# Hyena's output projection in the gates' rings: yh's split in hT's first half, the last two gate chunks as one group, two more gate chunks left for the attention

## The chip, the cores and the metric

The kernel runs on one core of a Trainium2 chip. The metric is the device time of one execution in microseconds (us), the median of several runs. The engines are PE (TensorE, matrix products), DVE (VectorE), ACT (ScalarE), POOL (GpSimd) and SP (SyncE, which here only issues DMAs). All data are fp32; the large products are each made of three passes over halves of a split operand (hi and lo).

## The reference

One block over 1024 latent tokens of width 1024, with 256 context tokens. Cut to what matters:

```python
h = modulate(rmsnorm(x, norm1_g), sh1, sc1)
q, k, v, hv, hx1, hx2, gna, ghy = split(h @ w_in)          # 5120 columns = 40 chunks of 128
y_na = neighbourhood_attention(q, k, v, k_ctx, v_ctx, rpb)
y_hy = hyena_mixer(hv, hx1, hx2, ...)                      # filters, then 2 long convolutions
m = sigmoid(gna) * (y_na @ w_na_o) + sigmoid(ghy) * (y_hy @ w_hy_o)
x = x + g1 * (m @ w_out)
x = x + g2 * swiglu(modulate(rmsnorm(x, norm2_g), sh2, sc2))
return rmsnorm(x, final_g)
```

Chunks 0 to 3 of the input projection are q, 4 to 11 k and v, 12 to 23 the Hyena inputs, 24 to 31 the gate gna, 32 to 39 the gate ghy.

## The kernel before

Everything is held with features on the 128 partitions and tokens along the free axis; a chunk is 128 features by 1024 tokens, done in two halves of 512 tokens. hT is the normed input, split into hTh and hTl, 8 x 128 features by 1024 tokens.

*Input projection* (`project`, L562). Per half of a chunk there are 24 matmuls (`gemm`, L186: 8 slices of features by three passes) into a bank `in_ps`, an eviction by ACT into a tile `proj` (a ring of two), and after the second half a store to DRAM, for a gate the scratch `gate`. Chunk weights are loaded (`weights`, L177: one raw buffer `wr`, two split pairs `wh`, `wl`) one chunk ahead.

*Side phase* (L946). The 40 chunks are the filler of a generator `side` that holds the Hyena filters (`filters`, L336: four sets, each of four steps that load decay tiles `dec`, multiply on PE into `filt_ps` and scale on DVE into `fv`, and then transforms `dft_ps`), the rows of the modulation (`ada_rows`, `ar_ps`), and four convolutions (`conv`, L437: DVE butterflies, PE transforms `dft_ps`). `_merged` (L138) picks by weights: side has SIDE = 447 steps against 39 for the projection, so a larger SIDE gives fewer chunks by the time that side ends. When the last convolution is reached, `fine` makes the projection go in halves.

*Attention* (`attention`, L649). 32 items (a pair of heads by 8 x 16 windows of the latent grid) in a pipeline: PE makes scores `s_ps` of item n, transposes the weights of item n-1 (`pt_ps<-ident,pe`) and multiplies the values of item n-2 (`pt_ps<-pts,v`); DVE and ACT make the softmax between. The biases of an item's scores are two loads of 192 KB on SP into four buffers. First AHEAD = 5 halves of chunks go alone, then each item is followed by one half of what is left (L959), twelve halves, items 0 to 11.

*Hyena's output projection* (`hyena_out`, L823). After the last half, hT's pool and the projection's weights are closed, and new pools take their place: `wf`, `ya`, `hyo` and one bank `ps1`. The Hyena output yh comes back from DRAM as eight loads `yhraw` of 256 KB, through a ring of two buffers (tag g), and is split into yhh and yhl. Then 16 halves (8 chunks f by 2) of 12 matmuls `hy_ps`, each multiplied by the stored gate (`ghy`, 256 KB loaded to the same ring) and stored to the scratch `hyo`. L978 says which items of the attention get one: not items 12 to 14, and from then on three of four.

*Mix* (`mix`, L1026). For each of eight chunks f: 2 x 12 matmuls `na_ps`, the gates `gate` and `hyo` loaded and combined into mh, ml; and the output weight `wor` (512 KB), multiplied by the row g1. Two chunks at a time go through `out_ps`. The eight x tiles are loaded behind the second chunk's gates. Its pools w4 and w4b stand on the side where the attention's stood.

Each engine runs its instructions in the order in which the program was written, except where a scheduler moves instructions ahead by priority; SP's queue is one order of all loads, and a load waits at its head until its buffer is free.

Of the kernel before, what the change touches and what calls it, by code (L numbers as in the profile page):

```python
# [18 lines left out]
P = 128  # L19
# [4 lines left out]
SIDE = 447  # L24
# [134 lines left out]
class Block:  # L159
# [17 lines left out]
    def weights(self, pool, src, n=D, tag="w"):  # L177
        nc = self.nc
        raw = pool.tile([P, n], F32, tag=tag + "r", name=tag + "r")
        nc.sync.dma_start(raw, src)  # L180
        hi = pool.tile([P, n], F32R, tag=tag + "h", name=tag + "h")
        lo = pool.tile([P, n], F32R, tag=tag + "l", name=tag + "l")
        self.split(hi, lo, raw)
        return hi, lo
# [74 lines left out]
    def hidden(self, pool, wpool, mp, hid, w3, hT, hcT, psf):  # L259
# [42 lines left out]
        self.modulated(pool, psf, xs[0:4], 4, self.mod1[:, 0], hT[0][:, :, 0:512], hT[1][:, :, 0:512])  # L302
        normed(4, 4, "rstd1b")
        yield
        self.modulated(pool, psf, xs[4:8], 4, self.mod1[:, 0], hT[0][:, :, 512:T], hT[1][:, :, 512:T])
# [256 lines left out]
    def project(self, groups, wpool, psg, psc, hT, hcT, between):  # L562
# [8 lines left out]
        def half(f, w, st, ps, h):  # L571
# [4 lines left out]
            self.gemm(pt, w, hT, 8, 512, h * 512, self.pinned)  # L576
# [50 lines left out]
        for group in groups:  # L627
            ws = [self.ready.pop(f) for f in group]
            i = chunks.index(group[-1]) + 1
            if i < len(chunks) and chunks[i] not in self.ready:  # L630
                with self.tc.high_priority():
                    self.ready[chunks[i]] = self.weights(wpool, self.a["w_in"][chunks[i]])
            sts = [self.stg.tile([P, T], F32, tag="o", name="proj") for _ in group]
            pss = [[] for _ in group]
            for h in range(2):
                for f, w, st, ps in zip(group, ws, sts, pss):
                    half(f, w, st, ps, h)
                if self.fine and not h:
                    yield
                if group is groups[0]:  # L640
                    next(between)
            for f, w, st in zip(group, ws, sts):
                self.left -= 1
                finish(f, w, st)
                yield
# [240 lines left out]
    def run(self):  # L886
        tc, nc, a = self.tc, self.nc, self.a
        with ExitStack() as top:
# [74 lines left out]
            with ExitStack() as s3:  # L963
# [7 lines left out]
                with ExitStack() as s4:  # L971
# [8 lines left out]
                    for _ in hyena:  # L980
                        pass
# [447 lines left out]
```

## Time and profile before

| what | value |
|---|---|
| time, median of 3 runs | 1749.97 us (1749.7 to 1755.51) |
| the profiled execution | 1746.28 us, its span 1744.5 us |
| PE busy | 1671.1 us, 96% of the span |
| DVE, ACT, POOL busy | 1187.9, 661.6, 157.9 us |
| granted PE clock, mean | 0.989 |
| filters, modulation rows | to about 303 us |
| convolutions beside chunks | 303 to 686 us |
| attention with input chunks, then Hyena chunks | 696 to 948 us |
| mix and FFN | 948 us to the end |

The stages are read from the first and last starts of their tiles. A busy time counts instructions that run on the engine, not the time in which it waits; an engine at 96% leaves 73 us in which it stands idle, over all stages. The table says nothing of where these are; the rows below do.

### The profile page before, as it was taken

The numbers are of one execution on the slowest core, as the hardware profiler recorded it, in microseconds if no ns is written. First come the engines' busy times: TensorE is split into PE (matmuls) and PEld (weight loads), VectorE is DVE, ScalarE is ACT, GpSimd is POOL, SyncE is SP. The second block draws the span as 40 slices with busy tenths as digits, with TensorE's granted clock in tenths as the row PEclk, the third lists the DMA queues.
The fourth block names the chain that finished last, engine by engine and source line by source line (L and its number), as shares of the span: only waits on it lengthen the run. The fifth ranks groups of instructions, "written<-read, shape, count | busy, mean of one in ns | idle before, by whom it ended". The sixth has DMA issues, their size and how long they took to land.

```text
span 1744.5 us, 22924 instructions
## 1 busy us (share of the span) xinstructions
PE 1671.1 (96%) x8348; PEld 1315.6 (75%) x8348; DVE 1187.9 (68%) x2004; ACT 661.6 (38%) x1143; POOL 157.9 (9%) x281
## 2 busy tenths in 40 slices
PE   5999999999999999998999999899999999999997
PEld 2766766777777777787777888688888888877886
DVE  4556266699795855655965867968765656479567
ACT  4611222312221213545654225633343333344555
POOL 0100210101000004002200000000100000100000
PEclk8999999999999999999999999999999999999999
DMA  8376556645454427435747524233423322395344
GB/s 344 116 248 199 182 180 222 210 147 179 138 203 160 160 100 223 135 109 165 218 146 247 167 67 168 110 116 126 139 91 101 103 98 97 108 374 180 99 121 151
DMA packets 110758, 281.20 MB, mean 161 GB/s; under 512 B 15535, under 2 KB 24371, under 8 KB 108341
## 3 DMA queue, kind: packets, MB, share of 16 engines
q1 hardware_dynamic: 90584, 218.68, 37.9%
q0 software_dynamic: 19408, 60.61, 10.2%
q8 instruction: 66, 1.08, 0.3%
q10 hardware_dynamic: 653, 0.44, 0.1%
q14 instruction: 47, 0.39, 0.1%
HBM read 212.28 MB, written 67.39 MB: 160 GB/s over the span
## 4 chain that ended last, share of the span: by engine, by line
PE 67%; issue 13%; DMA 9%; DVE 6%; ACT 3%; POOL 1%; SPq 0%; ACTq 0%; POOLq 0%; DVEq 0%
PE in_ps L194 22%; PE x_ps L1133 9%; PE dx_ps L1297 5%; PE dft_ps L430 5%; PE z_ps L1133 4%; PE out_ps L1071 4%; PE dz_ps L1297 3%; PE dft_ps L431 2%; PE dft_ps L432 2%; PE na_ps L194 2%; DMA w<-in_w 2%; DMA wal<-in_w_ada 2%; PE y_ps L1133 1%; PE dy_ps L1297 1%; PE ctx_ps L194 1%
## 5 line engine op out<-in xcount | busy, mean ns | idle before, releaser
L194 PE MATMUL in_ps<-hTh,wl 128*128 128x512 f32 x640 | 257.8, 404 | 3.6 <-ACT proj L601 3.6
L194 PE MATMUL in_ps<-hTl,wh 128*128 128x512 f32 x640 | 252.7, 395 | 0.0
L194 PE MATMUL in_ps<-hTh,wh 128*128 128x512 f32 x640 | 252.2, 395 | 0.0
L194 PEld LDWEIGHTS in_ps<-hTh,wl 128*128 128x128 f32 x640 | 121.3, 190 | 34.8 <-issue 5.9
L194 PEld LDWEIGHTS in_ps<-hTh,wh 128*128 128x128 f32 x640 | 121.2, 189 | 26.8 <-issue 1.2
L194 PEld LDWEIGHTS in_ps<-hTl,wh 128*128 128x128 f32 x640 | 121.3, 189 | 25.6 <-issue 1.2
L175 DVE TENSOR_TENSOR wl<-wr,wh 128x1024 fp32r<-128x1024 f32 x40 | 48.9, 1222 | 80.4 <-ACT wh L174 80.2
L175 DVE TENSOR_TENSOR ol<-ws,oh 128x512 fp32r<-128x512 f32 x88 | 60.6, 689 | 55.1 <-ACT oh L174 54.9
L174 ACT CAST wh<-wr 128x1024 fp32r<-128x1024 f32 x40 | 41.9, 1047 | 139.4 <-PE in_ps L194 111.2
L175 DVE TENSOR_TENSOR ol<-ar,oh 128x512 fp32r<-128x512 f32 x77 | 53.0, 689 | 49.0 <-ACT oh L174 49.0
L174 ACT CAST oh<-ar 128x512 fp32r<-128x512 f32 x77 | 47.9, 622 | 84.0 <-PE dx_ps L1297 34.7
L174 ACT CAST oh<-ws 128x512 fp32r<-128x512 f32 x88 | 54.7, 622 | 54.3 <-PE x_ps L1133 23.9
L1297 PE MATMUL dx_ps<-ol,oh 128*128 128x512 f32 x176 | 68.7, 391 | 1.7 <-DVE ol L175 1.7
L1297 PE MATMUL dx_ps<-oh,ol 128*128 128x512 f32 x176 | 67.1, 391 | 3.3 <-DVE ol L175 3.3
L754 DVE CUSTOM_DVE_ANT_0 pe<-s_ps,bias 128x640 f32<-128x640 f32 x64 | 50.1, 819 | 29.1 <-PE s_ps L749 29.1
L1297 PE MATMUL dx_ps<-oh 128*128 128x512 f32 x176 | 68.5, 389 | 0.0
L430 PE MATMUL dft_ps<-a,matf 128*128 128x512 f32 x128 | 66.1, 598 | 1.8 <-issue 1.1
L175 DVE TENSOR_TENSOR ol<-wr,oh 128x512 fp32r<-128x512 f32 x70 | 48.1, 690 | 28.8 <-ACT oh L174 28.7
L755 ACT ACTIVATE pe<-pe,mx 128x640 f32<-128x640 f32 x64 | 52.6, 823 | 37.5 <-DVE mx L754 37.4
L174 ACT CAST oh<-wr 128x512 fp32r<-128x512 f32 x70 | 43.1, 621 | 55.3 <-PE y_ps L1133 18.2
L1073 DVE TENSOR_TENSOR x<-x,out_ps 128x512 f32<-128x512 f32 x64 | 43.1, 685 | 18.7 <-PE out_ps L1071 18.5
L358 DVE TENSOR_TENSOR fv<-filt_ps,dec 128x512 f32<-128x512 f32 x32 | 21.6, 690 | 48.4 <-DMA dec<-in_decay 30.7
(392 smaller groups left out, 4225.4 us busy)
## 6 DMA issues: line engine op xcount, KB each, us to landing
wr<-in_w SPq DMA_DIRECT2D x50, 512.0 KB, 3.4
wr<-in_w_in SPq DMA_DIRECT2D x40, 512.0 KB, 4.5
ar<-g SPq DMA_DIRECT2D x77, 256.0 KB, 2.8
wal<-in_w_ada SPq DMA_DIRECT2D x32, 512.0 KB, 4.8
g<-t POOLq DMA_DIRECT2D x49, 256.0 KB, 3.0
matf<-in_dft_f SPq DMA_DIRECT2D x32, 384.0 KB, 4.3
bias<-in_rpb SPq DMA_DIRECT2D x64, 192.0 KB, 3.1
w<-in_w SPq DMA_DIRECT2D x44, 256.0 KB, 5.4
```

Of the source, the lines that this page charges most:

```text
L174: self.nc.scalar.copy(hi, src)
L175: self.nc.vector.tensor_sub(lo, src, hi.bitcast(F32))
L194: mm = nc.tensor.matmul(ps, ww[:, k * P:(k + 1) * P], xx[:, k, pos:pos + width], start=(i == 0), stop=(i == n - 1))
L430: nc.tensor.matmul(ps, m[:, 0], v.rearrange("p a b -> p (a b)"), start=True, stop=False)
L431: nc.tensor.matmul(ps[:, 0:256], m[:, 1], v[:, 1], start=False, stop=False)
L432: nc.tensor.matmul(ps[:, 256:512], m[:, 2], v[:, 0], start=False, stop=True)
L754: nc.vector.tensor_tensor_reduce(pe, ps[:, 256:896], bt, -1.0, 3e38, ALU.add, ALU.min, mx[:, 0:1])
L755: nc.scalar.activation(pe, pe, AF.Exp, bias=mx[:, 0:1], scale=-1.0, accum_out=mx[:, 1:2])
L1071: nc.tensor.matmul(ps, gg[x][:, tk], ww[y][:, sl], start=(i == 0), stop=(i == n - 1))
L1073: nc.vector.tensor_add(x1[:, sl], x1[:, sl], ps)
L1133: mm = nc.tensor.matmul(ps, w[u][:, k * P:(k + 1) * P], x[v][:, k, :], start=(start and k == 0 and i == 0), stop=(stop and k == 3 and i == 2),
L1297: nc.tensor.matmul(ps[j], x[u][:, j * P:(j + 1) * P], w[v], start=(start and i == 0 and c == 0), stop=(stop and i == N - 1 and k == len(re ...
```

## The change

1. hT is two tiles, one for each 512 tokens, in two pools: h1 (tokens 512 to 1023) and h0 (tokens 0 to 511).
2. The last two gate chunks, 30 and 31, form one group: first halves of both, then second halves of both. After the first halves nothing reads h0 any more, and `then` starts the loads of yh into h0's place, under the second halves.
3. `yhraw` goes through the ring of `tm` in the staging pool (two buffers), the gate of a Hyena chunk through the ring of `proj`, as one load of 512 KB (`ghy`), and is stored as one of 512 KB. The weights of Hyena's chunks and of `na_ps` go through the input weights' ring, `hy_ps` through the bank of `in_ps`.
4. ya, the attention's output split, is put where h1 was; pools `wf`, `hyo`, `ps1` fall away, and g1 gets a pool of its own that opens after the last Hyena half.
5. Each attention item from the one after the last gate half on gets one Hyena half, until there are none.
6. SIDE is 483: the chunks are spread more thinly over the steps of side, and four halves more are left for the attention, sixteen in all (items 0 to 15) beside the five alone.

The diff, cut to its core:

```diff
-SIDE = 447
+SIDE = 483
...
-            self.gemm(pt, w, hT, 8, 512, h * 512, self.pinned)
+            self.gemm(pt, w, hT[h], 8, 512, 0, self.pinned)
...
             for h in range(2):
                 for f, w, st, ps in zip(group, ws, sts, pss):
                     half(f, w, st, ps, h)
-                if self.fine and not h:
-                    yield
+                    if self.fine:
+                        if h:
+                            self.left -= 1
+                            finish(f, w, st)
+                        yield
                 if group is groups[0]:
                     next(between)
-            for f, w, st in zip(group, ws, sts):
-                self.left -= 1
-                finish(f, w, st)
-                yield
+                if group is groups[-1] and not h:
+                    then()
...
-    def hyena_out(self, pool, wo, ps1):
+    def hyena_out(self, pool, wpool, ps1):
...
-        yh = [pool.tile([P, 4, T], F32R, name=n, bufs=1) for n in ("yhh", "yhl")]
+        yh = [pool.tile([P, 8, 512], F32R, tag=n, name=m).rearrange("p (c h) t -> p c (h t)", h=2)
+              for n, m in (("hTh", "yhh"), ("hTl", "yhl"))]
         for c in range(4):
             for h in range(2):
                 sl = slice(h * 512, (h + 1) * 512)
-                raw = pool.tile([P, 512], F32, tag="g", name="yhraw")
+                raw = self.stg.tile([P, 4, P], F32, tag="tm", name="yhraw").rearrange("p a b -> p (a b)")
                 nc.sync.dma_start(raw, self.yhd[c][:, sl])
                 self.split(yh[0][:, c, sl], yh[1][:, c, sl], raw)
         yield
+        w = self.weights(wpool, a["why"][0], 512)
         for f in range(8):
-            w = self.weights(wo, a["why"][f], 512, "wf")
+            g = self.stg.tile([P, T], F32, tag="o", name="ghy")
+            nc.sync.dma_start(g, self.gd[8 + f])
             for h in range(2):
                 sl = slice(h * 512, (h + 1) * 512)
-                ps = ps1.tile([P, 512], F32, tag="f", name="hy_ps")
+                ps = ps1.tile([P, 512], F32, tag="g", name="hy_ps")
                 self.gemm(ps, w, yh, 4, 512, h * 512, True)
-                g = pool.tile([P, 512], F32, tag="g", name="ghy")
-                nc.sync.dma_start(g, self.gd[8 + f][:, sl])
-                nc.vector.tensor_tensor(g, ps, g, op=ALU.mult)
-                nc.gpsimd.dma_start(self.hyd[f][:, sl], g)
+                nc.vector.tensor_tensor(g[:, sl], ps, g[:, sl], op=ALU.mult)
+                if h:
+                    nc.gpsimd.dma_start(self.hyd[f], g)
+                    if f < 7:
+                        w = self.weights(wpool, a["why"][f + 1], 512)
                 yield
...
-                order = [[4, 5]] + [[f] for f in list(range(6, 24)) + list(range(4)) + list(range(32, 40)) + list(range(24, 32))]
+                order = [[4, 5]] + [[f] for f in list(range(6, 24)) + list(range(4)) + list(range(32, 40)) + list(range(24, 30))]
+                order.append([30, 31])
...
+                self.ya = [t.rearrange("p (c h) t -> p c (h t)", h=2) for t in new(h1, "ya")]
+                for _ in attention:
+                    next(hyena, None)
+                for _ in hyena:
+                    pass
+                att.close()
...
-                    for n, _ in enumerate(attention):
-                        if n > 2 and n % 4 != 3 or n in (3, 19):
-                            next(hyena, None)
...
-                            last = self.mix(wp, wf, mp, psf, g1, x1)
+                            last = self.mix(wp, wpool, mp, psf, g1, x1)
```

How the instructions stand on the engines at three places, before and after (the number at a row's start is its place on that engine).

PE at the fourth set of filters. Before:

```order
749 L432 MATMUL dft_ps<-a,matf 128x256
750 L351 MATMUL filt_ps<-fw_272,hid 128x256 x12
751 L194 MATMUL in_ps<-hTh,wl 128x512
...
799 L557 MATMUL tm_ps<-ident,proj 128x128 x4
800 L865 MATMUL ar_ps<-wal,cs 32x256 x4
801 L351 MATMUL filt_ps<-fw_272,hid 128x256 x3
802 L557 MATMUL tm_ps<-ident,proj 128x128 x4
803 L351 MATMUL filt_ps<-fw_272,hid 128x256
804 L865 MATMUL ar_ps<-wal,cs 32x256 x4
```

The three dots hold one whole chunk, 48 matmuls `in_ps`, between the third and the fourth step. After:

```order
750 L432 MATMUL dft_ps<-a,matf 128x256
751 L351 MATMUL filt_ps<-fw_277,hid 128x256 x12
752 L877 MATMUL ar_ps<-wal,cs 32x256 x4
753 L351 MATMUL filt_ps<-fw_277,hid 128x256
754 L877 MATMUL ar_ps<-wal,cs 32x256
755 L351 MATMUL filt_ps<-fw_277,hid 128x256 x3
756 L877 MATMUL ar_ps<-wal,cs 32x256 x3
757 L194 MATMUL in_ps<-hTh,wl 128x512
```

The four steps (16 matmuls `filt_ps`) follow each other with only modulation rows between; the chunk comes behind them. The third set stands likewise.

SP at the loads of yh. Before, the pairs alternate with the biases of an item's scores and a Hyena weight:

```order
250 L696 DMA kcraw<-kc_115 128x256
251 L831 DMA yhraw<-yh_100 128x512 x2
252 L180 DMA wfr<-in_why 128x512
253 L736 DMA bias_5146<-in_rpb 128x384
254 L736 DMA bias_5147<-in_rpb 128x384
255 L831 DMA yhraw<-yh_101 128x512 x2
256 L736 DMA bias_5148<-in_rpb 128x384
257 L736 DMA bias_5149<-in_rpb 128x384
258 L831 DMA yhraw<-yh_102 128x512
259 L180 DMA wfr<-in_why 128x512
260 L831 DMA yhraw<-yh_102 128x512
261 L736 DMA bias_5146<-in_rpb 128x384
```

After, the first two `yhraw` loads have gone long before, in the last convolution, and six stand here:

```order
260 L744 DMA bias_5034<-in_rpb 128x384
261 L840 DMA yhraw<-yh_101 128x512
262 L744 DMA bias_5031<-in_rpb 128x384
263 L744 DMA bias_5032<-in_rpb 128x384
264 L840 DMA yhraw<-yh_101 128x512
265 L840 DMA yhraw<-yh_102 128x512 x2
266 L840 DMA yhraw<-yh_103 128x512 x2
267 L744 DMA bias_5033<-in_rpb 128x384
268 L744 DMA bias_5034<-in_rpb 128x384
269 L846 DMA ghy<-gate_223 128x1024
```

Five of them stand together, with two bias loads ahead of them and two behind.

SP at the first loads of the mix. Before, with two gate halves of Hyena still to come (`ghy`), the first output weight `wor` and the first gates go ahead of them:

```order
318 L1033 DMA wor<-in_wout 128x1024
319 L1043 DMA gate<-gate_215 128x512
320 L841 DMA ghy<-gate_230 128x512
321 L1044 DMA gate<-hyo_203 128x512
322 L1043 DMA gate<-gate_215 128x512
323 L1044 DMA gate<-hyo_203 128x512
324 L1033 DMA wor<-in_wout 128x1024
325 L180 DMA wfr<-in_wna 128x512
326 L841 DMA ghy<-gate_230 128x512
327 L1052 DMA x_4_8037<-in_x 128x1024
328 L1052 DMA x_0_8048<-in_x 128x1024
329 L1052 DMA x_1_8049<-in_x 128x1024
```

After, they stand behind the last Hyena gate, the last biases and the weights of two `na_ps` chunks:

```order
313 L846 DMA ghy<-gate_230 128x1024
314 L744 DMA bias_5033<-in_rpb 128x384
315 L744 DMA bias_5034<-in_rpb 128x384
316 L180 DMA wr<-in_wna 128x512 x2
317 L1040 DMA wor<-in_wout 128x1024
318 L1050 DMA gate<-gate_215 128x512
319 L1051 DMA gate<-hyo_203 128x512
320 L1050 DMA gate<-gate_215 128x512
321 L1051 DMA gate<-hyo_203 128x512
322 L1040 DMA wor<-in_wout 128x1024
323 L1059 DMA x_0_8017<-in_x 128x1024
324 L1059 DMA x_1_8018<-in_x 128x1024
```

The waits of the program show that this first `wor` load waits for the last store `hyo`, whose source lies where the load writes.

## Rows read from the trace of the kernel before

**Rows 1.** The page's part 1: busy time, share of the span, instructions.
```profile
PE 1671.1 (96%) x8348; PEld 1315.6 (75%) x8348; DVE 1187.9 (68%) x2004; ACT 661.6 (38%) x1143; POOL 157.9 (9%) x281
```

**Rows 2.** Busy times by stage: stretch, length, each engine's busy us, PEclk, DMA share, GB/s.
```profile
130.00:240.00 110.00, 102.92 (x575) 74.89 (x574) 54.71 (x71) 22.09 (x38) 14.25 (x25) 0.98 0.57 190
340.00:480.00 140.00, 140.00 (x595) 106.17 (x594) 127.02 (x227) 33.80 (x49) 12.63 (x17) 1.00 0.49 159
480.00:686.00 206.00, 206.00 (x873) 159.65 (x872) 147.53 (x241) 44.73 (x65) 22.29 (x40) 1.00 0.51 168
809.10:835.70 26.60, 20.02 (x181) 16.84 (x180) 19.76 (x47) 20.13 (x40) 1.12 (x2) 0.87 0.70 210
947.70:975.00 27.30, 27.30 (x121) 22.61 (x122) 20.80 (x30) 7.10 (x11) 0.54 (x1) 1.00 0.76 272
```

**Rows 3.** PE in order of time: start, us, line, operation [idle before <-releaser].
```profile
799.88 0.45 PE L746 MATMUL s_ps<-krh,qrl 64*128 64x384 f32 x2
...
809.12 0.45 PE L746 MATMUL s_ps<-krh,qrl 64*128 64x384 f32 x2
...
819.44 2.40 PE L766 MATMUL pt_ps<-ident,pe 128*128 128x128 f32 x10 [5.60 <-ACT yrow L787]
...
830.31 1.31 PE L766 MATMUL pt_ps<-ident,pe 128*128 128x128 f32 x10 [0.95 <-ACT yrow L787]
...
832.80 0.50 PE L194 MATMUL hy_ps<-yhh,wfl 128*128 128x512 f32 x1
...
835.74 0.44 PE L746 MATMUL s_ps<-krh,qrl 64*128 64x384 f32 x2
...
842.25 0.45 PE L746 MATMUL s_ps<-krh,qrl 64*128 64x384 f32 x2
...
947.67 0.47 PE L194 MATMUL na_ps<-yah,wfl 128*128 128x512 f32 x1 [0.88 <-DVE ghy L842]
```

**Rows 4.** SP's queue in order of time, same columns, at the first yhraw loads.
```profile
809.22 0.86 SPq L831 DMA_DIRECT2D yhraw<-yh  x2
...
813.65 4.71 SPq L831 DMA_DIRECT2D yhraw<-yh  x2
```

**Rows 5.** DMA issues by line: KB each, median us from issue to landing.
```profile
gate<-proj POOLq DMA_DIRECT2D x16, 512.0 KB, 3.8
...
yhraw<-yh SPq DMA_DIRECT2D x8, 256.0 KB, 3.2
```

**Rows 6.** DVE in order of time, second set of filters.
```profile
142.92 1.46 DVE L358 TENSOR_TENSOR fv<-filt_ps,dec 128x512 f32<-128x512 f32 x2 [3.46 <-DMA dec<-in_decay]
146.41 1.44 DVE L358 TENSOR_TENSOR fv<-filt_ps,dec 128x512 f32<-128x512 f32 x2 [2.02 <-DMA dec<-in_decay]
```

**Rows 7.** PE in order of time, same set.
```profile
143.67 1.90 PE L351 MATMUL filt_ps<-fw,hid 64*128 64x256 f32 x8 [2.77 <-DVE fv L358]
...
146.26 0.63 PE L194 MATMUL in_ps<-hTh,wh 128*128 128x512 f32 x1
146.69 0.63 PE L194 MATMUL in_ps<-hTh,wl 128*128 128x512 f32 x1
...
149.70 0.39 PE L194 MATMUL in_ps<-hTh,wh 128*128 128x512 f32 x1
...
155.82 0.39 PE L194 MATMUL in_ps<-hTh,wh 128*128 128x512 f32 x1
```

**Rows 8.** DVE in order of time, second convolution.
```profile
347.35 0.69 DVE L418 SCALAR_TENSOR_TENSOR a<-x,b 128x512 f32<-128x512 f32 x1
```

**Rows 9.** PE in order of time, same place.
```profile
348.14 1.09 PE L430 MATMUL dft_ps<-a,matf 128*128 128x512 f32 x2
```

**Rows 10.** SP's queue in order of time, first loads of the mix.
```profile
928.83 0.33 SPq L1033 DMA_DIRECT2D wor<-in_wout  x1
...
942.30 5.16 SPq L1052 DMA_DIRECT2D x<-in_x  x7
```

**Rows 11.** PE's instructions of the score tile: first and last start.
```profile
L746 PE MATMUL s_ps<-krh,qrl x64: 439/442/685, 695.9 to 927.6; 64*128 64x384 f32 x64
```

More of the change, by code (lines that the diff above doesn't have):

```diff
@@ L560, in tokens, with project @@
             nc.gpsimd.dma_start(dst[:, 4 * h:4 * h + m], st[:, :m])
-    def project(self, groups, wpool, psg, psc, hT, hcT, between):
+    def project(self, groups, wpool, psg, psc, hT, hcT, between, then):
         nc = self.nc
@@ L627, in project @@
         for group in groups:
+            i = chunks.index(group[-1]) + 1
+            for f in (*group, *chunks[i:i + 1]):
+                if f not in self.ready:
+                    with self.tc.high_priority():
+                        self.ready[f] = self.weights(wpool, self.a["w_in"][f])
             ws = [self.ready.pop(f) for f in group]
[L629 to L632, printed above, removed]
             sts = [self.stg.tile([P, T], F32, tag="o", name="proj") for _ in group]
@@ L907, in run @@
             self.setup(cpool)
+            rows = top.enter_context(ExitStack())
             with ExitStack() as s1:
-                E1 = s1.enter_context
-                hpool = E1(tc.tile_pool(name="hT", bufs=1))
-                hT = [hpool.tile([P, 8, T], F32R, name=n) for n in ("hTh", "hTl")]
-                wpool = _Bufs(E1(tc.tile_pool(name="w", bufs=2)), wr=1)
+                E0, E1 = rows.enter_context, s1.enter_context
+                h1 = E0(tc.tile_pool(name="hT1", bufs=1))
+                wpool = _Bufs(E0(tc.tile_pool(name="w", bufs=2)), wr=1)
+                h0 = E1(tc.tile_pool(name="hT0", bufs=1))
+                new = lambda p, m: [p.tile([P, 8, 512], F32R, tag=n, name=m + n[-1]) for n in ("hTh", "hTl")]
+                hT = [new(p, "hT") for p in (h0, h1)]
                 psg = [E1(tc.tile_pool(name="psg", bufs=1, space=PSUM))]
@@ L930, in run @@
                         next(hidden)
-                        proj = self.project(order, wpool, psg, psc, hT, hcT, hidden)
+                        hyena = self.hyena_out(h0, wpool, psg[0])
+                        proj = self.project(order, wpool, psg, psc, hT, hcT, hidden, lambda: next(hyena))
                         next(proj)
@@ L961, in run @@
                     next(proj)
+                self.ya = [t.rearrange("p (c h) t -> p c (h t)", h=2) for t in new(h1, "ya")]
[4 more added lines that the diff above has]
+                att.close()
             with ExitStack() as s3:
                 E3 = s3.enter_context
-                rows = ExitStack()
-                wf = _Bufs(rows.enter_context(tc.tile_pool(name="wf", bufs=2)), wfr=1)
-                yp = rows.enter_context(tc.tile_pool(name="ya", bufs=1))
-                g1 = yp.tile([P, D], F32, name="g1")
+                g1 = rows.enter_context(tc.tile_pool(name="g1", bufs=1)).tile([P, D], F32, name="g1")
                 nc.gpsimd.dma_start(g1, self.modd[2].broadcast_to((P, D)))
-                self.ya = [yp.tile([P, 4, T], F32R, name=n) for n in ("yah", "yal")]
-                with ExitStack() as s4:
-                    E4 = s4.enter_context
-                    ps1 = E4(tc.tile_pool(name="ps1", bufs=1, space=PSUM))
-                    hp = E4(tc.tile_pool(name="hyo", bufs=2))
-                    hyena = self.hyena_out(hp, wf, ps1)
-                    next(hyena)
-                    for n, _ in enumerate(attention):
-                        if n > 2 and n % 4 != 3 or n in (3, 19):
-                            next(hyena, None)
-                    for _ in hyena:
-                        pass
-                    att.close()
                 psf = E3(tc.tile_pool(name="psf3", bufs=8, space=PSUM))
@@ L1030, in mix @@
         for f in range(8):
-            wn = self.weights(wo, a["wna"][f], 512, "wf")
+            wn = self.weights(wo, a["wna"][f], 512)
             raw = wp.tile([P, D], F32, tag="wor4", name="wor", bufs=2)
```

15 lines of the change are left out of this document (10 added, 5 removed).

## The prediction

> **What bounds the kernel now.** I read the page's busy times first. TensorE (PE) is busy for 1671.1 of 1744.5 us [rows 1], so the change can win only where PE stands idle or runs slowly, and by moving PE's work to where PE would otherwise stand. Next comes the table by stages [rows 2]. From 340 to 480 and from 480 to 686 us, in the convolutions, PE has no idle time at all, while VectorE (DVE) is busy for 127.02 of 140 us in the first of them and 147.53 of 206 in the second. From 130 to 240 us, the filters, PE is idle for 110.00 - 102.92 = 7.1 us. From 809.1 to 835.7 us, where the attention hands hT's room to the Hyena projection, PE is idle for 26.60 - 20.02 = 6.6 us at a mean clock of 0.87. Then I read PE's own order of time through the attention [rows 3]: an item with half an input chunk as filler takes 809.12 - 799.88 = 9.24 us, one with half a Hyena chunk 842.25 - 835.74 = 6.51 us. The largest hole is the 5.60 us before 819.44. Its releaser is named ACT yrow, but the transposes also needed scores whose bias load stands on SyncE's queue (SP) behind two yhraw loads, issued in a burst of 4.71 us from 813.65 [rows 4]; these waited for their ring of two.
>
> **The change, part by part.** All sums are made against the profiled execution, 1746.28 us (span 1744.5 and 1.8 around it). The median of the runs is 1749.97, 3.7 us above it; I add that at the end.
>
> *Filler taken from the side phase.* Two chunks, four halves, leave the stretch in which PE is 100% busy and go into the attention. A half is 24 matmuls; from 149.70 to 155.82 there are 27 steps [rows 7], 0.2267 us each, so a half is 5.44 us and four are 21.8. The side phase gets shorter by 21.8 us if PE stays its bound.
>
> *Attention.* Before, from item 12 to the first na_ps: 947.67 - 809.12 = 138.6 us, with two items that have no filler, others too, and the holes. After, items 12 to 15 carry the four halves, 4 x 9.24 = 37.0, and items 16 to 31 one Hyena half each, 16 x 6.51 = 104.2. Then come the two steps that only drain the pipeline: transposes and values are 832.80 - 830.31 = 2.5 us, values alone about 1.5 [rows 3], which I round up to 4.2 for both. That is 145.4, so +6.9 (with rounding). It already counts every hole of before from 809 to 947 as gone. Together with the first term the change gains 14.9 us if no new wait appears; three terms give some back.
>
> *X, loading yh.* It now runs under items 14 and 15 instead of in the open. Eight loads of 256 KB go through a ring of two, and a load takes 3.2 us to land [rows 5]; with the split of two behind it I estimate 4.5 us for a pair and 18 for the four pairs. Two items and the first part of the third are 18.5 + 3.9 = 22.4 us, so it fits by about 4. The order shows that the first of them even stands before the bias loads of one item. But six yhraw loads stand in a row on SP, each waiting for its ring, and two bias loads behind them: what is late next is a score's bias. Low bound 0.5 (all hidden), high bound 5 (most of the 5.60 us hole again); I take 1.5, nearer to the low one, because there is filler now where there was none.
>
> *Y, the side phase with less filler.* The order shows that the last two sets of filter steps no longer have an input chunk between them. What such a run costs is in the trace: DVE's steps fv come 146.41 - 142.92 = 3.5 us apart, waiting for decay loads [rows 6], and PE, which has banks for two steps ahead, stands 2.77 us before 143.67. The clock then falls: the matmuls from 146.26 to 146.69 are 0.43 us apart instead of 0.227 [rows 7], about eight of them, with the filter's own slow ones about 1.75 us. Two sets: 2 x (2.77 + 1.75) = 9.0. Against that, of the 7.1 us of idle time in 130 to 240 us the 4.3 outside this hole (waits for other loads and steps beside the same sets) are replaced: 9.0 - 4.3 = +4.7. In the convolutions I count nothing: the weights 483 to 447 spread the chunks 8% thinner, which takes some 7 us of PE's 140 off from 340 to 480 and leaves 133 against DVE's 127.02 [rows 2]. That is close; at 348.14 PE's transform starts 0.1 us after DVE's operand a (347.35 + 0.69) [rows 8, 9]. Bounds: 0 (the sets' waits merely replace the others) and 10, or much more, by the third rival.
>
> The Trainium skill (TensorE: Matmul & The Clock Gate, Part 1, "What's actually happening") says that the array has two rates, 1.2 and 2.4 GHz, and goes to the lower when it has been idle. The spacing behind the 2.77 us hole agrees, 0.43 against 0.227. By the rate alone, without the slow filter steps, Y would be 0.3 us less.
>
> *Z, the start of the mix.* Before, the first wout load was issued at 928.83, 18.8 us before na_ps starts, and the x loads at 942.30 [rows 10]. After, its tile lies in room that the stores of the Hyena chunks read from, so it waits for the landing of the last of them, 512 KB; stores of that size from the same queue land 3.8 us after issue [rows 5]. With the product before it, all mix loads behind it on SP (wout, gates, x) start about 5 us after the last Hyena half, when na_ps starts too (4.2). By hand from there: na_ps of two chunks, four halves of 12 x 0.2267 = 2.72, ends at 15.1; the first chunk's part of eight output tiles, 24 matmuls, at 20.6. The second chunk's first gates are complete when 4.2 MB have come (two wout, four gate halves of the first chunk, three x, in the order that stands on SP); at the 272 GB/s of the mix's start [rows 2] that takes 15.4 us, until 20.4, and sigmoid, product, sum and split, about 0.7 us each, until 23.2. PE waits some 2.5 us, and the clock costs 1.5 more: Z = +4. Bounds 1.5 (one short hole, the tiles in another order) and 9 (three more x loads, 1.6 MB or 5.8 us, ahead of those gates).
>
> For the store the Trainium skill (DMA: Bandwidth & Descriptors, "Anatomy of one DMA", where it gives a fit of 2.0 us plus bytes over 436 thousand) would say, as an estimate, 3.2 us for 512 KB. The row says 3.8, and the measurement decides; by the page Z would be 0.6 less.
>
> *At nothing:* hT in two halves (same matmuls), gates and stores of 512 KB in place of 2 x 256 KB (fewer issues, hidden behind an item), the Hyena weights in the input weights' ring (loaded an item ahead), one bank for hy_ps as before.
>
> Sum: 1746.28 - 21.8 + 6.9 + 1.5 + 4.7 + 4.0 = 1741.6 on the profiled execution, + 3.7 = 1745.3; I say **1745**.
>
> **The rivals.**
> *Full gain:* side phase still PE-bound, mix loads arriving in time: X 0.5, Y 0, Z 1.5, so -12.9, 1737. For it: no PE idle time from 340 to 686 us, and 58 us of DVE idle time in 480 to 686 to move into. Against it: the 2.77 us hole already stands in a filter set that lacks its chunk.
> *Late loads:* X 5 and Z 9 with Y 4.7: +3.8, 1754. For it: the 5.60 us hole is the same loads with the same ring on the same queue. Against it: 22.4 us of cover.
> *Slower: the side phase becomes DVE's.* PE's transforms already start 0.1 us after their operands in places; if DVE's chain with its loads, and not PE, sets the length of filters and convolutions, the chunks taken out leave holes of their own size. Y = 21.8 gives +12.4, 1762. It passes the time of before from Y = 9.4 on, and 0.5% above it from Y = 18. For it: 127 of 140 us. Against it: DVE had 13 us idle there, and 58 later.
> That the change does not do what it says is excluded: the order shows four halves in the attention and the loads under them.
>
> **How the numbers follow.** Forecast 0.50 (X, Y, Z near their values; by their bounds 1740 to 1751), full gain 0.25, late loads 0.12, DVE-bound 0.13. About 0.5%, 8.75 us, is what a measurement of this kernel can tell from no change: faster means below 1741.2, slower above 1758.7. Faster: 0.22 of the full gain and 0.08 of the forecast, 0.30. Slower: 0.09 of the DVE-bound case and 0.02 of late loads, 0.11. Within: 0.59. The range from 1736 to 1757 leaves out the best end of the full gain and most of the DVE-bound case, some 2 in 10.
>
> **What would show it.** The first s_ps should come about 17 us earlier than at 695.9 [rows 11] if Y is 4.7; 22 means Y = 0, under 5 the DVE rival. Holes of 2 to 4 us on PE before filt_ps in the third and fourth set show Y; new ones before dft_ps between 340 and 686 the DVE rival. No hole over 2 us on PE before the first hy_ps shows X; items of 9.24 and 6.51 us the attention's sum. One hole of 2 to 4 us before out_ps of the first pair, with wout and gate loads issued at or after the first na_ps, shows Z. The forecast is wrong if the first s_ps is less than 12 or more than 21 us earlier, or if more than 10 us are lost between the last score and the second pair of the mix.

## The result and the profile after

The changed kernel took 1754.99 us (median, 1749.58 to 1758.46) against 1748.76 us for the kernel before in the same runs: ratio 1.0037, interval 1.0023 to 1.0052. It is slower by about 6.5 us. Forecast was 1745, 5 us below the 1749.97 us that the forecast started from: the time lies inside the stated range, but it went the other way, and forecast and measured change lie some 11 us apart. (The profiled execution of after is 10 us above that of before, more than the medians differ; where that matters it is said.)

The page of the changed kernel, busy times:

```profile
PE 1682.8 (96%) x8348; PEld 1318.0 (75%) x8348; DVE 1186.3 (68%) x2004; ACT 659.9 (38%) x1143; POOL 154.2 (9%) x273
```

PE is busy 11.7 us longer than in [rows 1] for the same 8348 matmuls: its mean granted clock is 0.984 where it was 0.989. It runs at the lower clock behind new holes, and for longer in the first 118 us (0.90 there, 0.96 before). The stages, in the columns of [rows 2]:

```profile
130.00:240.00 110.00, 102.58 (x564) 75.29 (x564) 56.01 (x73) 19.11 (x33) 13.96 (x25) 0.97 0.57 186
240.00:303.00 63.00, 57.87 (x311) 39.78 (x310) 23.93 (x35) 15.15 (x25) 5.26 (x8) 0.97 0.58 187
...
340.00:480.00 140.00, 137.96 (x578) 103.92 (x576) 125.18 (x224) 33.28 (x48) 11.81 (x15) 0.99 0.49 162
480.00:680.00 200.00, 200.00 (x853) 154.83 (x852) 151.86 (x251) 46.16 (x69) 24.28 (x42) 1.00 0.53 174
809.00:842.50 33.50, 33.42 (x250) 27.11 (x248) 17.15 (x38) 18.13 (x35) 0.56 (x1) 1.00 0.40 122
947.00:980.00 33.00, 26.86 (x140) 21.02 (x139) 18.40 (x26) 11.03 (x17) 0.97 (x2) 0.95 0.86 301
```

From 240 to 303 us PE is idle for 5.1 us; the kernel before is idle for 1.5 there:

```profile
240.00:303.00 63.00, 61.47 (x321) 43.93 (x319) 37.23 (x53) 16.13 (x26) 6.65 (x9) 1.00 0.61 198
```

From 340 to 480 us there is a hole of 2.0 us where there was none. From 809 to 842.5 us, where yh is now loaded, PE has no hole to speak of: the 6.6 us of [rows 2] are gone. The start of the mix has holes of 6.1 us. The first score of the attention:

```profile
L754 PE MATMUL s_ps<-krh,qrl x64: 439/442/445, 690.2 to 940.0; 64*128 64x384 f32 x64
```

It comes 5.7 us earlier than in [rows 11]; 17.1 were forecast, and the prediction itself called less than 12 a sign of being wrong. The first `na_ps` stands at 952.17, so the attention takes 262.0 us from its first score, against 251.8 before. Here are the holes. The one in the second set of filters, known from [rows 7], is there as before, a little longer:

```profile
149.66 0.70 PE L351 MATMUL filt_ps<-fw,hid 64*128 64x256 f32 x2 [3.15 <-DVE fv L358]
```

DVE in the third set, in order of time:

```profile
200.69 1.29 DVE L358 TENSOR_TENSOR fv<-filt_ps,dec 128x512 f32<-128x512 f32 x2 [3.81 <-PE filt_ps L351]
...
207.07 1.34 DVE L358 TENSOR_TENSOR fv<-filt_ps,dec 128x512 f32<-128x512 f32 x2 [4.62 <-DMA dec<-in_decay]
210.50 0.69 DVE L358 TENSOR_TENSOR fv<-filt_ps,dec 128x512 f32<-128x512 f32 x1 [2.09 <-DMA dec<-in_decay]
```

and PE beside it:

```profile
207.81 1.96 PE L351 MATMUL filt_ps<-fw,hid 64*128 64x256 f32 x8 [3.50 <-DVE fv L358]
...
210.72 0.63 PE L194 MATMUL in_ps<-hTh,wh 128*128 128x512 f32 x1
211.15 0.63 PE L194 MATMUL in_ps<-hTh,wl 128*128 128x512 f32 x1
```

The steps `fv` are 6.4 and 3.4 us apart and wait for decay loads. PE, with no chunk between the steps, stands 3.50 us until DVE frees a bank, and then its matmuls are 0.43 us apart, as behind the hole of [rows 7]. The fourth set repeats it:

```profile
282.70 0.70 PE L351 MATMUL filt_ps<-fw,hid 64*128 64x256 f32 x2 [2.58 <-DVE fv L358]
```

In the second convolution, PE and then DVE:

```profile
423.76 0.50 PE L194 MATMUL in_ps<-hTh,wl 128*128 128x512 f32 x1 [1.97 <-DVE proj L588]
...
424.76 0.63 PE L194 MATMUL in_ps<-hTh,wl 128*128 128x512 f32 x1
425.18 0.63 PE L194 MATMUL in_ps<-hTl,wh 128*128 128x512 f32 x1
```

```profile
421.17 0.74 DVE L588 SCALAR_TENSOR_TENSOR proj<-in_ps,cw,proj 128x511 f32<-128x511 f32 x1
421.83 1.22 DVE L532 SCALAR_TENSOR_TENSOR yo<-yo,hx 128x1024 f32<-128x1024 f32 x1
422.96 0.75 DVE L588 SCALAR_TENSOR_TENSOR proj<-in_ps,cw,proj 128x512 f32<-128x512 f32 x1
```

PE waits 1.97 us for the bank of a Hyena input chunk, whose tap (`proj`, 0.75 us) DVE runs behind a product of the convolution (`yo`, 1.22 us), and pays for it with eight slow matmuls more. The start of the mix, SP and PE:

```profile
953.91 0.33 SPq L1040 DMA_DIRECT2D wor<-in_wout  x1
```

```profile
952.17 0.50 PE L194 MATMUL na_ps<-yah,wl 128*128 128x512 f32 x1 [0.36 <-ACT yrow L795]
...
964.06 0.50 PE L1078 MATMUL out_ps<-wouh,ml 128*128 128x512 f32 x1 [0.72 <-DVE ml L175]
...
969.58 0.50 PE L1078 MATMUL out_ps<-wouh,ml 128*128 128x512 f32 x1 [1.14 <-DVE gate L1053]
...
972.90 0.50 PE L1078 MATMUL out_ps<-wouh,ml 128*128 128x512 f32 x1 [2.36 <-DVE gate L1053]
```

The first `wor` load goes out after `na_ps` has begun (before: 18.8 us ahead, [rows 10]), and PE stands 0.72, 1.14 and 2.36 us before `out_ps`.

If the moved matmuls are counted at their own time, PE's delay against the kernel before is 5 us by 144 us, 12 at 285 us, 17 behind the hole at 423 us, 16 at the first score, 5 at the first `na_ps`, 11 behind the start of the mix and 10 at the end. (This delay is the difference of the same matmul's start in the two traces, with the matmuls that were moved past it taken off.) Some 4 us of it stand there at the first transform already, up to which PE runs the same 480 matmuls in both kernels but for two (117.2 against 112.9 us); e5 comes back to that:

```profile
L430 PE MATMUL dft_ps<-a,matf x128: 590/592/697, 117.2 to 621.3; 128*128 128x512 f32 x128
```

### The profile page after: what moved, and what is told of

It reads as the page before. It is cut to its first block, busy times and chain, and to the rows that moved or that the text cites. A ratio compares the mean times of both kernels' runs of the same rounds, so it can differ in the third digit from the quotient of the medians.

```text
span 1754.5 us, 22906 instructions
## 1 busy us (share of the span) xinstructions
PE 1682.8 (96%) x8348; PEld 1318.0 (75%) x8348; DVE 1186.3 (68%) x2004; ACT 659.9 (38%) x1143; POOL 154.2 (9%) x273
## 4 chain that ended last, share of the span: by engine, by line
PE 43%; issue 34%; DMA 9%; DVE 6%; POOL 4%; ACT 3%; SPq 0%; POOLq 0%; ACTq 0%; DVEq 0%
PE in_ps L194 15%; PE dx_ps L1304 5%; PE out_ps L1078 4%; PE dz_ps L1304 3%; PE dft_ps L430 3%; PE x_ps L1140 2%; PE dft_ps L431 1%; PE dft_ps L432 1%; DMA w<-in_w 1%; POOL g L1252 1%; PE dy_ps L1304 1%; PE pt_ps L774 1%; DMA wada<-in_w_ada 1%; POOL g L1246 1%; PE pt_ps L788 1%
## 5 line engine op out<-in xcount | busy, mean ns | idle before, releaser
L175 DVE TENSOR_TENSOR wl<-wr,wh 128x1024 fp32r<-128x1024 f32 (+1 forms) x56 | 59.8, 1068 | 82.6 <-ACT wh L174 82.3
L174 ACT CAST wh<-wr 128x1024 fp32r<-128x1024 f32 (+1 forms) x56 | 51.8, 925 | 153.5 <-PE in_ps L194 120.4
L1078 PE MATMUL out_ps<-wouh,ml 128*128 128x512 f32 x128 | 51.2, 400 | 5.2 <-DVE gate L1053 3.5
```

What stands on the lines that cost most here:

```text
L174: self.nc.scalar.copy(hi, src)
L175: self.nc.vector.tensor_sub(lo, src, hi.bitcast(F32))
L1078: nc.tensor.matmul(ps, gg[x][:, tk], ww[y][:, sl], start=(i == 0), stop=(i == n - 1))
```

## The experiments

All ratios are against runs of the kernel before on the same chip, with 95% intervals. Theory A: the filters lost their cover. Its rivals: the new layout costs (B), the attention or the mix costs (C, D), VectorE bounds the convolutions (E).

**e1_after_side447: the two chunks back in the side phase.**

```diff
-SIDE = 483
+SIDE = 447
```

> The changed kernel with SIDE = 447 as before: the new rings and the loads of yh in hT's first half stay, only the two chunks go back to the side phase. Theory A (the loss comes from the filler taken out of the filters and convolutions, the new rings themselves cost nothing): the first s_ps comes where it did before, 695.9 us, give or take the 5 us by which runs differ in their first 110 us; the 5.60 us hole before the first Hyena half is gone, and since the Hyena halves end at item 27 the first wout load goes out 15 us or more before na_ps. From item 12 on 16 x 6.51 + 4 x 3.6 + 4.2 = 123 us against 138.6, with some 4 us of small waits: about -11 us, 1738, ratio 0.994. Rival B (the layout costs: rings shared by chunks, gates and yh): new PE holes in the side phase with the old filler too, and a ratio of 1.000 or more. Rival C (the loss sits in the attention and the mix alone): the gain is the same -11 but the side phase shows no difference to the changed kernel's.

Measured: 1743.82 us, ratio 0.9964 (0.9950 to 0.9979). The layout alone wins 6 us, so B falls, and so does C, since the side phase does differ. The first score:

```profile
L754 PE MATMUL s_ps<-krh,qrl x64: 439/442/445, 700.9 to 932.9; 64*128 64x384 f32 x64
```

It comes 5.0 us later than before, of which some 3 stand at the first transform already; from there to the first `na_ps` it is 244.3 us against 251.8, a gain of 7.5 where A expected 11: four items without filler wait for ACT. Undoing the chunks alone brings 0.73%, 13 us.

**e2_before_side483: the two chunks out of the kernel before.**

```diff
-SIDE = 447
+SIDE = 483
```

> The kernel before with SIDE = 483 alone: two chunks fewer beside filters and convolutions, nothing else changed. Theory A: PE waits 3 us and more in each of the last two filter sets and again in the second convolution, first s_ps only some 6 to 11 us earlier than 695.9 in place of 21.8; the attention keeps its 5.60 us hole and gets longer by 21.8 less what its unfilled items give back: +8 to +11 us, 1757 to 1760, ratio 1.005 to 1.006. Rival B (layout): first s_ps 17 to 22 us earlier, ratio 1.000.

Measured: 1779.55 us, ratio 1.0165 (1.0144 to 1.0185), far above what A expected. The side phase has the holes of the changed kernel (2.43 and 2.17 us before `filt_ps` in the third and fourth sets, 1.85 us in the second convolution), and the first score, at 693.3 us, comes only 2.6 us earlier than before; A expected 6 to 11. The attention takes 31.7 us longer than before. PE in order of time:

```profile
850.08 2.39 PE L766 MATMUL pt_ps<-ident,pe 128*128 128x128 f32 x10 [4.59 <-ACT yrow L787]
...
864.83 2.39 PE L766 MATMUL pt_ps<-ident,pe 128*128 128x128 f32 x10 [4.60 <-ACT yrow L787]
```

```profile
961.75 0.50 PE L194 MATMUL hy_ps<-yhh,wfl 128*128 128x512 f32 x1 [2.19 <-DVE ghy L842]
...
976.79 0.50 PE L194 MATMUL na_ps<-yah,wfl 128*128 128x512 f32 x1 [2.60 <-DVE ghy L842]
```

With fewer items left, the loads of yh and the last Hyena halves stand in the open: two holes of 4.6 us at the start, and at the end Hyena halves without an item beside them, most of them waiting for their gate. So leaving chunks for the attention needs the new layout, and the layout does not need the chunks.

**e3_after_stgkeep: the first `wor` load no longer behind the last store.**

```diff
+                self.stg = E0(tc.tile_pool(name="stg", bufs=2))
                 h0 = E1(tc.tile_pool(name="hT0", bufs=1))
...
-                self.stg = E1(tc.tile_pool(name="stg", bufs=2))
```

> The changed kernel with the staging pool (rings of gates and yh) kept open through the mix and put below hT's first half, so that the first wout load no longer waits for the last store of a Hyena chunk. Theory A (Z, the late loads of the mix, is 6 us of the loss): the first wout and gate loads are issued 4 to 5 us earlier, PE's three holes before out_ps (0.72, 1.14, 2.36 us) shrink to one at most, -4 us: 1751, ratio to before 1.001. Rival D (the mix's loads are bound by the bandwidth of the transfers, not by when they start): the holes stay and the ratio stays at 1.004.

Measured: 1755.69 us, ratio 1.0033 (1.0020 to 1.0046): nothing that can be told from the changed kernel. The load went out 8 us earlier, and the holes before `out_ps` were gone, but another came. SP, ACT and PE:

```profile
945.84 0.33 SPq L1040 DMA_DIRECT2D wor<-in_wout  x1
```

```profile
952.92 0.63 ACT L1052 ACTIVATE gate<-gate 128x512 f32<-128x512 f32 x1 [1.98 <-DMA gate<-gate]
953.46 0.25 ACT L795 COPY yrow<-pt_ps 128x128 f32<-128x128 f32 x1
```

```profile
953.76 0.80 PE L194 MATMUL na_ps<-yah,wl 128*128 128x512 f32 x1 [2.75 <-ACT yrow L795]
```

ACT's sigmoid, now ahead of the last copy of the attention's output (`yrow`), waits for its gate, and PE for the copy. One wait took the place of another.

**e4_after_dec4: four buffers for the decay tiles.**

```diff
-                        dec.append(pool.tile([P, 512], F32, tag="dec", name="dec", bufs=2))
+                        dec.append(pool.tile([P, 512], F32, tag="dec", name="dec", bufs=4))
```

> The changed kernel with four buffers for the decay tiles in place of two, so that the loads of two filter steps can run ahead. Theory A1 (the holes of 3.15, 3.50 and 2.58 us before filt_ps are the decay loads): the holes of all sets shrink to under 1 us and the first s_ps comes 6 to 8 us earlier than in the changed kernel, ratio to before 1.000. Rival A2 (they come from PE's banks and DVE's order): the holes stay, ratio 1.004.

Measured: 1742.13 us, ratio 0.9959 (0.9942 to 0.9975), 0.78% or 13.6 us under the changed kernel (with the two intervals, 10 to 17), more than A1 expected. DVE in the third set:

```profile
192.52 1.29 DVE L358 TENSOR_TENSOR fv<-filt_ps,dec 128x512 f32<-128x512 f32 x2 [3.81 <-PE filt_ps L351]
...
194.74 1.29 DVE L358 TENSOR_TENSOR fv<-filt_ps,dec 128x512 f32<-128x512 f32 x2 [0.47 <-PE filt_ps L351]
198.70 1.34 DVE L358 TENSOR_TENSOR fv<-filt_ps,dec 128x512 f32<-128x512 f32 x2 [2.67 <-DMA dec<-in_decay]
201.33 1.37 DVE L358 TENSOR_TENSOR fv<-filt_ps,dec 128x512 f32<-128x512 f32 x2 [1.28 <-DMA dec<-in_decay]
```

The second step follows the first by 2.2 us in place of 6.4, and no hole before `filt_ps` in this set is left on PE. A2 falls. The first score comes 15.7 us earlier than in the changed kernel:

```profile
L754 PE MATMUL s_ps<-krh,qrl x64: 439/441/445, 674.5 to 925.6; 64*128 64x384 f32 x64
```

With the moved matmuls taken off, about 10 us of that stand by 144 us, in the second set (half of it is the changed kernel's late start), and by 348 us it is 16; the hole of 2 us in the second convolution stands in both.

**e5_before_again: the kernel before, unchanged.** There is no edit.

> The kernel before once more, unchanged, for its trace. The changed kernel's PE was 4.8 us behind by 113 us, where the two programs do not differ. Theory A: that is what executions of one program differ by, so this trace stands 0 to 5 us off the first one at its first transform (112.9 us) and agrees with it from there to 686 us within 2 us. Rival: this trace has its first transform within 1 us of 112.9; then the 4.8 us belong to the changed kernel.

Measured: 1748.17 us, one run. From the first transform to 596 us the two traces of the kernel before agree within some 2 us.

```profile
L430 PE MATMUL dft_ps<-a,matf x128: 590/592/697, 113.6 to 627.9; 128*128 128x512 f32 x128
```

Its first transform stands at 113.6 us, 0.7 off the first trace, which by itself speaks for the rival. The other traces say otherwise in part. The changed kernel's program up to there, with only the staging pool's place changed, stood at 114.1 in e3 and 113.1 in e10, but at 117.2 in the first trace, 116.2 in e1 and 117.1 in e9. The profiled executions of those three took 1.3, 1.0 and 6.4 us more than their kernels' medians, those of before, e3 and e10 1.6 to 2.5 us less than theirs. So the profiled execution of before was a quick one, and part of the profiled 10 us is that. Whether the pools' places or the executions make the late start isn't settled.

**e6_before_dec4: four decay buffers in the kernel before.** The edit is that of e4, in the kernel before.

> The kernel before with four decay buffers in place of two. In the changed kernel that brought 13.6 us (1755.7 to 1742.1). Theory A1 (the change makes the filters wait for decay loads since the chunks that covered them are gone): here only the one open set (2.78 us and its slow clock) and the start are at stake, -3 to -6 us, ratio 0.997. Rival A3 (the loads cost the same with and without the change): -11 us or more, ratio 0.993 or less; then the change itself did not turn the loads into a bound.

Measured: 1747.98 us, ratio 0.9996 (0.9981 to 1.0011). Nothing, less than even A1 expected, although its trace too is 5 us ahead by 144 us. By 303 us 2 are left of them. The hole of [rows 7] is gone, but others come: one of 3.10 us where the first trace has none, and one of 3.21 us, where it has 1.98, for a load of the modulation rows.

```profile
157.87 1.12 PE L430 MATMUL dft_ps<-a,matf 128*128 128x512 f32 x2 [3.10 <-issue]
...
220.33 1.08 PE L865 MATMUL ar_ps<-wal,cs 128*32 128x256 f32 x8 [3.21 <-DMA wal<-in_w_ada]
```

The same edit is worth 13.6 us in the changed kernel and nothing here: it is the change that made the decay loads a bound. A3 falls. Not all of the 13.6 us is the missing chunks, though: in the new layout with the chunks in place (e1 against e7, below) the edit still brings 5 us.

**e7_after_dec4_side447 and e8_after_dec4_side465: four buffers, and no chunk or one chunk left.** The edit of e4, with SIDE = 447 or 465.

> The changed kernel with SIDE = 447 and four decay buffers. Theory A1 with A: the gains of both, as far as they do not repair the same holes: against the changed kernel with 447 (ratio 0.9964) another 3 to 6 us, ratio 0.994. Rival A3: another 11 us or more, ratio 0.990 or less.

> The changed kernel with SIDE = 465, one chunk left instead of two, and four decay buffers. By the sums a chunk in the attention is paid 10.9 us in the side phase where PE is its bound. Theory A (with the loads covered, the only hole left by the thinner filler is the one in the second convolution, 1.97 us and its slow clock, and it is there at 483 and not at 447): between 447 and 483 with four buffers, ratio 0.994 to 0.996. Rival: the number of chunks left does not matter once the loads are covered: all three within 2 us.

Measured: 1737.69 us, ratio 0.9933 (0.9914 to 0.9953), and 1735.45 us, 0.9933 (0.9912 to 0.9955); with e4 that is 0.9933, 0.9933, 0.9959 for no, one and two chunks left. The first scores stand at 691.6, 682.1 and 674.5 us, so a chunk taken out gives 9.5 and 7.6 us; the attention takes 243.5, 253.7 and 263.2 us, so a chunk put in costs 10.2 and 9.5. With the loads covered a moved chunk wins nothing that these runs can tell: none and one are equal (within some 5 us), two are 0.26% worse, at the edge of the intervals. So one chunk came out just under theory A's 0.994 to 0.996, and the rival's 2 us hold for none and one alone. With no chunk left, four buffers bring 0.31%, 5 us, over e1 (other chip), as A expected and not A3.

**e9_filters_dense: both chunks out of the convolutions, none out of the filters.** Two decay buffers, four halves left as in the changed kernel.

```diff
-SIDE = 483
+SIDE = 500
...
-                        yield from _merged((fgen, 97), (self.ada_rows(fp, psf), 26))
+                        for n in _merged((fgen, 97), (self.ada_rows(fp, psf), 26)):
+                            yield n * SIDE / 447
```

> The changed kernel with the same four halves left for the attention, but both chunks taken out of the convolutions: beside the filters the chunks stand as in the kernel before (the filters' steps are weighted by SIDE / 447, SIDE is 500). Two decay buffers as in the changed kernel. Theory A1 (most of the loss are the filter sets that lost their chunk): at 303 us it is as far as the kernel before, within 3 us, the holes of 3.50 and 2.58 us are gone. Theory A4 (in the convolutions two chunks can go at the price of the one hole of 2 us and its clock): first s_ps 16 us or more earlier than in the kernel before, ratio 0.996 to 0.999. Rival E (VectorE sets the length of the convolutions once they lose two chunks): several new holes before dft_ps or in_ps that wait for DVE, first s_ps less than 12 us earlier, ratio 1.001 or more.

Measured: 1741.93 us, ratio 0.9967 (0.9948 to 0.9985), 0.70% under the changed kernel. The stages, and the first score:

```profile
240.00:303.00 63.00, 60.45 (x319) 43.19 (x317) 38.02 (x56) 15.65 (x25) 6.06 (x8) 1.00 0.63 205
303.00:669.00 366.00, 365.84 (x1573) 278.45 (x1571) 295.20 (x504) 87.95 (x128) 41.09 (x67) 1.00 0.53 175
```

```profile
L754 PE MATMUL s_ps<-krh,qrl x64: 439/441/445, 679.8 to 931.2; 64*128 64x384 f32 x64
```

From 303 to 669 us PE is idle for 0.16 us: the convolutions gave up two chunks without one hole, with DVE busy for 295.20 of 366 us. The holes of 3.50 and 2.58 us in the filters are gone too, as A1 expected. E falls, and so does the fear that 1.97 us of hole goes with thinner filler there: that hole hangs on which chunk meets which step of the convolution. The first score is 16.1 us earlier than before, 20 if the 4 us of its late start are left out. Layout, buffers and the number of chunks moved are those of the changed kernel, so its loss hangs on where the chunks were taken from.

**e10_stgkeep_pinned: e3, and the first chunk's sigmoids behind the attention's copies on ACT.**

```diff
-                nc.scalar.activation(ga[:, 0], ga[:, 0], AF.Sigmoid)
+                sg = nc.scalar.activation(ga[:, 0], ga[:, 0], AF.Sigmoid)
+                if f == 0:
+                    self.tc.keep_in_program_order(sg)
```

> The changed kernel with the staging pool kept open, as in the run that freed the first wout load, and the first chunk's sigmoids pinned behind the attention's last copies on ACT. In the run without the pin the three holes before out_ps were gone, but ACT waited for a gate load ahead of the last yrow copy and PE stood 2.75 us before na_ps. Theory A (Z is real, 4 to 6 us, and the sigmoid took its place): neither hole stands, -4 us against the changed kernel, ratio 1.001 to 1.002. Rival D (transfers bound the start of the mix whatever the order): a hole of 2 us and more stays somewhere between 945 and 985 us, ratio 1.003 to 1.004.

Measured: 1753.12 us, ratio 1.0037 (1.0021 to 1.0053). The start of the mix, in the columns of the stages:

```profile
945.00:985.00 40.00, 37.76 (x192) 30.72 (x191) 28.13 (x39) 14.76 (x21) 1.07 (x2) 0.96 0.83 295
```

In this trace PE is idle for 2.2 us between 945 and 985 us, 1.55 of it a wait for the last values that the changed kernel's trace has too; there it was 6.1 in the same 40 us. The holes are gone, and the ratio has not moved. The two do not fit: either they cost less in most executions than in the one profiled (in e4, whose program is the same there, the holes before the first pair's `out_ps` are 0.90 and 0.36 us), or something came back that one trace does not show. Z is not shown in the time; by the intervals it is worth under 4 us.

**e11_dec4_465_pinned: e8 with the sigmoids pinned.** The edits of e8 and the pin of e10.

> The changed kernel with SIDE = 465, four decay buffers, and the first chunk's sigmoids pinned behind the attention's last copies on ACT. Without the pin (ratio 0.9933) ACT's sigmoid waited for a gate load with the copy of the last values behind it, and PE stood 1.49 and 3.99 us. Theory: the 3.99 us hole goes, -3 to -4 us, ratio 0.991. Rival: the load or the table load of the sigmoid comes late for the first product instead, a hole before out_ps takes its place, ratio 0.993.

Measured: 1734.20 us, ratio 0.9920 (0.9901 to 0.9940), the fastest of all, though its interval overlaps that of e8. PE in e8, and then in e11:

```profile
933.85 0.66 PE L788 MATMUL pt_ps<-pts,vc 128*64 128x128 f32 x8 [3.99 <-ACT yrow L795]
```

```profile
934.47 0.66 PE L788 MATMUL pt_ps<-pts,vc 128*64 128x128 f32 x8 [1.55 <-ACT yrow L795]
...
952.16 0.50 PE L1080 MATMUL out_ps<-wouh,ml 128*128 128x512 f32 x1 [1.87 <-DVE ml L175]
```

The 3.99 us hole fell to the usual 1.55, and a hole of 1.87 us before `out_ps` came: part of each expectation.

**e12_dense_dec4_pinned: e9, four decay buffers and the pin.** The edits of e9, e4 and e10's pin.

> Everything that helped, together: the changed kernel with both chunks taken out of the convolutions alone (as in the run with dense filters, ratio 0.9967), four decay buffers, and the first chunk's sigmoids pinned on ACT. Theory: with chunks beside the filters the decay loads are mostly covered already, so four buffers bring less than the 13.6 us that they brought to the changed kernel, 3 to 6 us, as they did with SIDE = 447 (0.9964 to 0.9933): ratio 0.992 to 0.994, and two chunks left are no better than one (0.992), since a chunk moved from a stretch where PE is full to another where it is full gains nothing. Rival (the gains add up): 0.989 or less.

Measured: 1739.69 us, ratio 0.9946 (0.9922 to 0.9969), a little short of what the theory expected. The gains do not add up, and two chunks left are not better than one. No hole before `filt_ps` that waits for DVE is left in the filters, but as in e6 others stand there, of 3.60 us before `dft_ps` and of 4.01 us for a load of the modulation rows.

## Why the prediction was wrong, point by point

*What bounds the kernel* was read rightly: PE, and the hole at 813.84. It is closed, and there is nothing in its place: from 702 to 846 us PE has no hole over 0.2 us. From first score to `na_ps` the attention got 10.2 us longer; forecast were 6.9 and X's 1.5, so 1.8 us less.

*Filler taken from the side phase, -21.8*: right as a count. In e9, where no hole is new, the first score comes 20 us earlier, its late start left out.

*But the account was set up wrongly.* The 14.9 us that the forecast put down to removing the two chunks and then filling the attention belong mostly to the layout: the closed hole and the filled items. By the same sum with no chunk moved, 12 halves as filler and four items of 3.6 us without, the layout alone gives about 11 (e1's expectation), and measured 6.3. The chunks could have won some 4 us more at most, and they carried all of Y's risk. A chunk that leaves a stretch where PE is full for another where PE is full won nothing here (e7, e8, e4). The forecast should have priced the two edits apart.

*Y, forecast +4.7, is the step that failed.* From the first transform to the first score PE's delay grew by 11 us in the first trace, by 13 and 14 in those of e3 and e10 and by 18 in that of e2, which have the same order of filters and chunks; and the three runs that repair it in different ways (e1, e4, e9) win back 12 to 14 us, each give or take 4. That is most of the 11 us between forecast and measurement, or all of it. The mechanism was right and was named with its rows: [rows 6, 7] show the hole that repeats, and in e4 and e9 the repeats are gone. The size was wrong in two places. First, the filters, which cost some 8 us in the first trace: 4.3 us of other waits were to be replaced by the new holes, but only some 2.5 were. (Before, PE is idle for 8.6 us from 130 to 303 us, 5.8 of them outside the hole of [rows 7]; after, for 12.5, of which the three holes of 3.15, 3.50 and 2.58 leave 3.3.) In the other three traces the filters cost 11 to 13 us; there the granted clock from 200 to 225 us is 0.80 to 0.86, against 0.93 in the first trace and 1.00 before. Second, the convolutions were counted at nothing: there the one hole at 421.8 us with its slow matmuls costs some 4 (1.97 and eight times 0.2 us). The upper bound of 10 went with the third rival, "VectorE's", and that rival named the wrong resource: the loads and their two buffers bound the filter sets, and the convolutions had room (e9).

*The stated bounds* do not fit each other: with X, Y and Z all at their lower or all at their upper bounds the sum runs from 1737 to 1759, not from 1740 to 1751.

*Z, forecast +4*: the mechanism is in the trace as told (`wor` behind the last store, holes before `out_ps`), 6 us of delay in the profiled execution. The stores of 512 KB took 4.0 us in the median (forecast 3.8 from [rows 5]), the last, issued at 947.63 just behind the load of g1, 6.1: it landed at 953.77, and `wor` went out at 953.91. The estimate from the fit of the Trainium skill (DMA: Bandwidth & Descriptors, "Anatomy of one DMA"), 3.2 us, is below all eight. Taking the wait away (e3, e10) moved no time that can be measured. So the term was too large, or its place was taken; that stays open.

*The rival "late loads"* came nearest in time (1754) and for a wrong reason: X was small.

*The two rates*: behind the holes of 3.50 and 1.97 us the matmuls are 0.43 us apart, against 0.227 elsewhere. That agrees with the two rates of the Trainium skill (TensorE: Matmul & The Clock Gate, Part 1). How Y was counted by them made 0.3 us of difference.

## What to carry to other kernels

Filler between the steps of a load-bound stage is also the time in which its loads land: before chunks are moved, look at which steps stood next to them, and how many buffers the loads there have. Price a move of work between two stretches by what either stretch has idle: from full to full it won nothing here, and its risk was all on the giving side. When an edit has two halves, a new layout and a new share of work, make the sum for each alone; here the layout alone was a gain (0.9964), and with four decay buffers, one chunk moved and the sigmoids pinned 0.9920.

## What the runs showed of the hardware

The low clock can follow a hole of 2 us, and need not. Behind the 1.97 us before 423.76 the first two matmuls still came 0.34 and 0.24 us apart, and the next eight 0.43, so that this hole cost nearly twice its length; e2 shows the same behind 1.85 us. But in e3 the same matmul waits 2.25 us, and behind it they come 0.23 us apart:

```profile
423.95 0.50 PE L194 MATMUL in_ps<-hTh,wl 128*128 128x512 f32 x1 [2.25 <-DVE proj L588]
...
424.52 0.40 PE L194 MATMUL in_ps<-hTh,wh 128*128 128x512 f32 x1
424.75 0.40 PE L194 MATMUL in_ps<-hTh,wl 128*128 128x512 f32 x1
```

From 420 to 440 us the mean granted clock is 0.91 in the changed kernel's trace and 1.00 in that of e3. What decides between the two isn't shown. So one price for every hole, as Y had it, is a guess.

And one trace is one execution: the profiled one lay between 3.9 us below (e6) and 6.4 above (e9) the median of its kernel, and e9's start, 4 us late by 117 us, was still 5 late at 596 us. Differences of two single traces below some 5 us can't be taken here for differences of the kernels.
